# A token difference taken from DRAM in place of a second subtraction in the up projection

## The chip, the cores and the metric

One Trainium2 chip, of which the program uses one core. The core's engines work side by side, each through its own row of instructions: TensorE (PE; its weight loads are listed apart as PEld), VectorE (DVE), ScalarE (ACT), GpSimd (POOL) and SyncE (SP), which here only issues transfers (DMAs). The metric is the device time of one execution in microseconds (us), lower is better.

## The reference

The kernel computes one decoder layer on S = 512 tokens of width D = 1024, all in float32: an RWKV-7 time mix, a sparse attention (compressed, selected and window branches), and a gated feed-forward part of width F = 2816 with a short convolution over the tokens. Only the last part is touched by the change. In short form:

```python
h = rmsnorm(x, norm_ffn)              # 512 x 1024
p = h @ W_up                          # 512 x 5632: gates and values
u = causal_conv(p, taps=3) + bias     # over the tokens
y = silu(u[:, :F]) * u[:, F:]         # 512 x 2816
out = x + rmsnorm(y @ W_down, g)      # 512 x 1024
```

## The kernel before

**Numbers.** TensorE multiplies in a reduced format. So each float32 operand is split into a high part (a copy by ACT) and a low part (operand minus high part, by DVE or POOL), and each product is three: high x high, low x high, high x low.

**Up projection.** `W_up` is cut into 44 blocks of 128 columns, which the loop takes as 22 pairs `j` (a gate and a value block). Pairs 0 to 9 are plain products. Pairs 10 to 21 (the tuple `SEVEN`) are computed by `seven(j)`: a 2 x 2 block product from seven products in place of eight, whose weight sums are made ahead and whose results `sg` and `sv` are put together by additions on DVE (`add`, L1572) from TensorE's sums `st`, `su` and so on. The weights for all this come from DRAM (`sw...r`, L168), are split by ACT (L134) and by DVE or POOL (L172), and lie in a pool `sw` with rings of buffers (`sraw` has four).

Behind each pair come the convolution (L1619 to L1621), the gate, the product `y` (L1635), and its split into `ah[:, j]` (ACT, L1638) and `al[:, j]` (DVE, L1639), two tiles that stay in SBUF for the down projection. `lft` and `rgt` are tokens 0 to 255 and 256 to 511.

**Down projection.** It, too, is a 2 x 2 block product from seven (L1749, `down`): the blocks are the two halves of the tokens by the first and last 11 pairs (`KH` = 11). It needs differences of `y` between the blocks. The first, T1 = `y[rgt] - y[lft]` for pairs 0 to 10, takes the place of `y[rgt]` in the up loop (L1637), before the split; so `ah` and `al` hold T1's high and low part. For pairs 11 to 21 the loop then makes T2 = `y[rgt] - T1` of the pair 11 earlier and T4 = `y[lft] - T2`. T2 takes two subtractions, of T1's high part (L1647) and of its low part (L1648), T4 one (L1649). Both lie in one tile `t24` (two buffers in a pool `t2`) and are stored to DRAM, `t24d` (pairs 11 to 20 by SP, L1645, one iteration later; pair 21 by POOL, L1652). The down projection loads them back as `t` (`load` in `turn`, L1706).

**Down weights.** `down_w` (L1655) loads the weights in the order in which they are used, `dw0`, `dw1`, ...: a load (L1668, SP), a high part (L1668, ACT) and a low part (L1669; POOL for n = 1, 4, 7, 10, ..., DVE otherwise). From n = 3 on the parts are `hh` and `hl`, eight slots. The first ten are started before the up loop is done. Behind them the pools `t2`, `sw` and others are closed, and a pool `ep` opens on the same memory. A tile of `ep` waits for the last use of the tile that lay there. `dw10r` to `dw13r` are the first loads in it. From n = 10 on `keep` pins the order in which loads and splits stand in each engine's row; the rest is put in order by a scheduler.

Of the kernel before, what the change touches and what calls it, by code (L numbers as in the profile page):

```python
# [10 lines left out]
F32 = mybir.dt.float32  # L11
F32R = mybir.dt.float32r
AF = mybir.ActivationFunctionType
OP = mybir.AluOpType
# [14 lines left out]
SEVEN = (10, 11, 12, 13, 14, 15, 16, 17, 18, 19, 20, 21)  # L29
SGRP = 2  # L30
UPOS = {j: i for i, j in enumerate(SEVEN + tuple(sorted(set(range(22)) - set(SEVEN))))}
RB = 4
KH, TL = 11, 4
# [19 lines left out]
def hybrid_layer(ctx: ExitStack, tc: tile.TileContext, a, out, dbg=None, stop=None):  # L53
# [3 lines left out]
    def pool(name, side="left", c=None):  # L57
        p = tc.tile_pool(name=name, bufs=1, side=side, reuse_waits="tile")
        if c is None:
            return p  # L60
        return c.enter_context(p)
# [192 lines left out]
    def weight_sums():  # L254
        gs = [group_sums(x, f) for x, f in zip(SGROUPS, fsum)]
        for i in range(0, len(gs), 4):
            for _ in range(8):
                for y in gs[i:i + 4]:
                    next(y)
                    yield  # L260

    t24d = dr.tile([KH, 128, S], F32, name="t24d", bufs=1)
    dsum = [[dr.tile([k.stop - k.start, 128, 512], F32, name=f"ds{i}{k.start}", bufs=1) for i in range(4)] for k in DCH]

# [1214 lines left out]
    with pool("ff") as ff:  # L1479
# [11 lines left out]
        def token_forms():  # L1491
            with pool("tr", "left") as tr_:
                raws = [{(r, n): tr_.tile([128, 2, 256], F32, tag=f"tr{r}{n}", name=f"tr{c}{r}{n}", bufs=1)
                         for r in range(2) for n in range(2)} for c in range(2)]

                def load(c, r, n):
                    ks = slice(2 * c, 2 * c + 2)
                    keep(ve.tensor_tensor(raws[c][r, n], quarter(h2h, r, n)[:, ks].bitcast(F32),
                                          quarter(h2l, r, n)[:, ks].bitcast(F32), op=OP.add))

                def diff(c, o, x, y):
                    keep(ve.tensor_tensor(raws[c][o], raws[c][x], raws[c][y], op=OP.subtract))

                def high(c, i, o):
                    keep(sc.activation(forms[i][0][:, 2 * c:2 * c + 2], raws[c][o], AF.Copy))

                def low(c, i, o):
                    keep(ve.tensor_tensor(forms[i][1][:, 2 * c:2 * c + 2], raws[c][o],
                                          forms[i][0][:, 2 * c:2 * c + 2].bitcast(F32), op=OP.subtract))

                for c in range(2):
                    load(c, 0, 1)
                    load(c, 0, 0)
                    diff(c, (0, 0), (0, 1), (0, 0))
                    yield
                    high(c, 0, (0, 0))
                    load(c, 1, 1)
                    diff(c, (0, 1), (0, 1), (1, 1))
                    yield
                    high(c, 2, (0, 1))  # L1520
                    low(c, 0, (0, 0))
                    diff(c, (1, 1), (1, 1), (0, 0))
                    load(c, 1, 0)
                    yield
                    high(c, 1, (1, 1))
                    low(c, 2, (0, 1))
                    diff(c, (1, 0), (1, 0), (1, 1))
                    yield
                    high(c, 3, (1, 0))
                    low(c, 1, (1, 1))  # L1530
                    low(c, 3, (1, 0))
                    yield
            yield
# [10 lines left out]
            return hi, lo  # L1544

        def form_seq():
            for j in SEVEN:
                n = SEVEN.index(j)
                fs = [f[n % SGRP] for f in fsum[n // SGRP]]
                for x, eng in (((0, 0), po), (2, po), (1, ve), (3, po), ((0, 1), po), (4, po), ((1, 1), ve)):  # L1550
                    src = fs[x - 1] if isinstance(x, int) else a["up4"][x[0], x[1], UPOS[j]]
                    ahead.append(form_w(src, f"sw{j}{x if isinstance(x, int) else 5 + 2 * x[0] + x[1]}", eng))
                    yield
# [4 lines left out]
        def seven(j):  # L1558
# [29 lines left out]
            add(v[:, lft], t[1][:, rgt], u2)  # L1588
            return g, v

        side = token_forms()
        sctx2 = ExitStack()
        for j in range(22):
            us = []
            sv_ = None
            if j == 2:
                sw = pool("sw", "right", sctx2)
            if j == SEVEN[0]:
                for _ in side:
                    pass  # L1600
            if j in SEVEN:
                sv_ = seven(j)
            for x in range(2):
                blk = 2 * j + x
                if blk < NU:
                    p = pu4[blk]
                    half_up(blk, 1)
                elif sv_ is not None:
                    p = sv_[x]
                else:  # L1610
                    wh, wl = after.get(blk) or split_w(upw(blk), f"up{blk}")
                    p = ((pj, px, py, pz)[blk % 4] if j < SEVEN[0] else pj)(f"pu{blk}")
                    mm3(p, wslice(wh), wslice(wl), lambda k: h2h[:, k, :], lambda k: h2l[:, k, :])
                if blk == 2 * SEVEN[0] - 1:
                    for _ in range(5):
                        next(coming)
                cv = blk * 4
                u = fu.tile([128, S], F32, tag=f"u{x}", name=f"u{blk}", bufs=2)
                sc.activation(u, p, AF.Identity, scale=cvec[:, cv + 2:cv + 3], bias=cvec[:, cv + 3:cv + 4])  # L1619
                ve.scalar_tensor_tensor(u[:, 1:], p[:, :S - 1], cvec[:, cv + 1:cv + 2], u[:, 1:], op0=OP.mult, op1=OP.add)  # L1620
                ve.scalar_tensor_tensor(u[:, 2:], p[:, :S - 2], cvec[:, cv:cv + 1], u[:, 2:], op0=OP.mult, op1=OP.add)  # L1621
                us.append(u)
                if j < SEVEN[0]:
                    for _ in range(1):
                        next(side, None)
                if (j > 2 or x == 0 if j < SEVEN[0] else x == 0 and j < 19):
                    next(ws, None)
            if sv_ is None:
                sc.activation(us[0], us[0], AF.Silu)
                (ve if j > SEVEN[0] - 3 else po).tensor_tensor(us[1], us[0], us[1], op=OP.mult)  # L1630
                y = us[1]
            else:
                sc.activation(sv_[0], us[0], AF.Silu)
                y = sv_[1] if j >= KH else us[1]
                ve.tensor_tensor(y, us[1], sv_[0], op=OP.mult)  # L1635
            if j < KH:
                ve.tensor_tensor(y[:, rgt], y[:, rgt], y[:, lft], op=OP.subtract)  # L1637
            sc.activation(ah[:, j, :], y, AF.Copy)  # L1638
            ve.tensor_tensor(al[:, j, :], y, ah[:, j, :].bitcast(F32), op=OP.subtract)  # L1639
            if j >= KH:  # L1640
                if j == KH:
                    t2ctx = ExitStack()
                    t2 = pool("t2", "left", t2ctx)
                else:
                    sy.dma_start(t24d[j - 1 - KH], t24)  # L1645
                t24 = t2.tile([128, S], F32, tag="t24", name=f"t24{j}", bufs=2)
                ve.tensor_tensor(t24[:, lft], y[:, rgt], ah[:, j - KH, rgt].bitcast(F32), op=OP.subtract)  # L1647
                ve.tensor_tensor(t24[:, lft], t24[:, lft], al[:, j - KH, rgt].bitcast(F32), op=OP.subtract)  # L1648
                ve.tensor_tensor(t24[:, rgt], y[:, lft], t24[:, lft], op=OP.subtract)  # L1649
            if j == 1:  # L1650
                f4ctx.close()
# [3 lines left out]
        def down_w(f, k):  # L1655
            n = next(ring)
            src = a["down4"][f[0], f[1], k] if isinstance(f, tuple) else dsum[k // 2][f][k % 2]
            if n < WB:
                hi, lo = (wp.tile([128, 512], F32R, tag=t, name=f"dw{t}{n}", bufs=WB) for t in ("whi", "wlo"))
            else:  # L1660
                hi, lo = (y[:, (n - WB) % 8, :] for y in (h2h, h2l))
            if n < 8 or n > 9 and n % 8 < 2 or n % 8 >= 6:
                raw = wp.tile([128, 512], F32, tag="raw", name=f"dw{n}r", bufs=RAWB)
            elif n < 10:
                raw = t2.tile([128, 512], F32, tag="draw", name=f"dw{n}r", bufs=2)
            else:
                raw = ep.tile([128, 512], F32, tag="draw", name=f"dw{n}r", bufs=4)
            load, high = sy.dma_start(raw, src), sc.activation(hi, raw, AF.Copy)  # L1668
            low = (po if n % 3 == 1 else ve).tensor_tensor(lo, raw, hi.bitcast(F32), op=OP.subtract)  # L1669
            if n >= 10:  # L1670
                keep(load)
                keep(high)
                keep(low)
            return hi, lo
# [244 lines left out]
```

## Time and profile before

| what | value |
|---|---|
| median of three runs | 1137.72 us (1138.17, 1132.95, 1137.72) |
| the profiled execution | 1133.54 us |
| span of its trace | 1131.5 us |
| mean granted TensorE clock | 0.997 |
| instructions | 21237 |
| moved by DMA | 208.33 MB, 184 GB/s |

The up projection's pairs 11 to 21 lie between about 905 and 1029 us, and the down projection's first product starts at 1018.99. In rows of the profile L12 is line 12 of the kernel, `out<-in` the tiles with buffer numbers left out, `x3` a count. SPq, ACTq and so on are issues of DMAs by an engine's queue. A value in brackets behind a row is the idle time ahead of it and the instruction that ended it. A view of a line or a tile also gives the time from the issue of a DMA to its landing.

### The profile page before, as it was taken

Reading aid. Unit: us, or ns where it says so; the run is one execution under the profiler, and the core shown is the slowest. Engines: PE = TensorE matmul, PEld = TensorE weight load, DVE = VectorE, ACT = ScalarE, POOL = GpSimd, SP = SyncE. Lnnn points to the kernel's source line nnn. Section 1 sums busy time; section 2 is a strip of 40 time slices with the busy share of each in tenths; the row PEclk is TensorE's granted clock in tenths of the full one; section 3 lists DMA queues with packets and bytes.
Section 4 is the critical chain, followed back from the end, with each engine's and each line's share of the span. In section 5 each row is a group of like instructions: output and inputs, shape, how many; then the busy total and the mean of one; then the engine's idle time right before and its main releaser. Section 6 shows DMA issues by size and latency. Waiting matters only on the chain.

```text
span 1131.5 us, 21237 instructions
## 1 busy us (share of the span) xinstructions
PE 1110.3 (98%) x7704; PEld 909.6 (80%) x7704; DVE 750.4 (66%) x1432; ACT 639.2 (56%) x1258; POOL 613.5 (54%) x615
## 2 busy tenths in 40 slices
PE   9999999999999999999999999999999999999997
PEld 7888888877888887766666777888888899998885
DVE  4236664735666552597787754755785699997986
ACT  6447763554666434386675654543554576665554
POOL 4346674535666453566545543540578777753431
PEclk9999999999999999999999999999999999999999
DMA  7524468632666896516576465777568678968783
GB/s 256 144 81 124 141 166 217 182 104 86 182 146 172 235 242 216 132 48 194 171 218 181 127 149 166 231 240 220 136 185 202 207 263 227 266 181 302 228 283 113
DMA packets 117002, 208.33 MB, mean 184 GB/s; under 512 B 37025, under 2 KB 39905, under 8 KB 110754
## 3 DMA queue, kind: packets, MB, share of 16 engines
q1 hardware_dynamic: 93538, 144.05, 40.6%
q0 software_dynamic: 7504, 48.50, 18.4%
q10 hardware_dynamic: 15856, 14.42, 4.0%
q8 instruction: 61, 1.00, 0.4%
q14 instruction: 43, 0.35, 0.1%
HBM read 179.60 MB, written 72.35 MB: 223 GB/s over the span
## 4 chain that ended last, share of the span: by engine, by line
PE 87%; DVE 5%; DMA 3%; POOL 2%; issue 1%; ACT 1%; SPq 0%; DVEq 0%; POOLq 0%; ACTq 0%
PE st L1567 4%; PE sg L1567 3%; PE dn L1745 3%; PE dn L1746 3%; PE dn L1747 3%; PE gt L348 3%; PE o L1218 3%; PE gt L349 3%; PE gt L350 3%; PE pt L150 3%; PE ub L1276 3%; PE pu L234 2%; PE ub L1278 2%; PE pu L232 2%; PE pu L233 2%; PE ub L1277 2%
## 5 line engine op out<-in xcount | busy, mean ns | idle before, releaser
L1166 ACT ACTIVATE p<-p,stt 128x384 f32<-128x384 f32 (+3 forms) x128 | 70.6, 554 | 33.4 <-DVE stt L1164 30.8
L1164 DVE CUSTOM_DVE_ANT_0 p<-s,rh 128x384 f32<-128x384 f32 (+3 forms) x128 | 59.2, 484 | 21.5 <-PE s L1150 17.9
L1138 POOL TENSOR_SCALAR p<-p,stt 128x512 f32<-128x512 f32 (+1 forms) x64 | 39.3, 622 | 38.7 <-DVE stt L1131 24.5
L1746 PE MATMUL dn<-hl,ah 128*128 128x512 f32 x148 | 57.6, 389 | 0.0
L1747 PE MATMUL dn<-hh,al 128*128 128x512 f32 x148 | 57.6, 389 | 0.0
L1745 PE MATMUL dn<-hh,ah 128*128 128x512 f32 x148 | 57.2, 389 | 0.0
L150 PE MATMUL pt<-ident,p 128*128 128x128 f32 x320 | 44.3, 273 | 1.2 <-DVE p L1140 1.2
L1157 PE MATMUL s<-kst,qs 128*128 128x512 f32 (+1 forms) x128 | 38.8, 394 | 5.8 <-DVE stt L1164 5.6
L150 PEld LDWEIGHTS pt<-ident,p 128*128 128x128 f32 x320 | 37.8, 141 | 6.9 <-DVE p L1140 1.6
L1218 PE MATMUL o<-PT,vt 128*64 128x384 f32 (+3 forms) x256 | 41.0, 443 | 0.0
L1209 ACT ACTIVATE PT<-pt 128x512 f32<-128x512 f32 x48 | 27.5, 587 | 10.4 <-PE pt L150 10.3
L1157 PEld LDWEIGHTS s<-kst,qs 128*128 128x128 f32 x128 | 21.2, 189 | 15.0 <-DVE stt L1164 11.8
L1140 DVE TENSOR_SCALAR p<-p,stt 128x512 f32<-128x512 f32 (+1 forms) x64 | 32.3, 532 | 0.7
L1747 PEld LDWEIGHTS dn<-hh,al 128*128 128x128 f32 x148 | 27.8, 188 | 5.8
L1745 PEld LDWEIGHTS dn<-hh,ah 128*128 128x128 f32 x148 | 27.8, 188 | 5.8
L1746 PEld LDWEIGHTS dn<-hl,ah 128*128 128x128 f32 x148 | 27.8, 188 | 5.7
L1218 PEld LDWEIGHTS o<-PT,vt 128*64 128x64 f32 x256 | 16.3, 136 | 18.3 <-issue 16.0
L272 POOL DMA_DIRECT2D ds<-in_down_dram x36 | 25.6, 710 | 7.3 <-DMA ds<-ds 7.3
L1620 DVE SCALAR_TENSOR_TENSOR u<-pu,cvec,u 128x511 f32<-128x511 f32 x20 | 15.0, 748 | 19.2 <-ACT u L1619 19.2
L1211 DVE COPY PT<-pt 128x512 f32<-128x512 f32 x32 | 21.8, 680 | 8.6 <-PE pt L150 8.5
L251 POOL DMA_DIRECT2D fs<-in_up_dram x36 | 26.0, 731 | 0.5 <-issue 0.4
L868 ACT ACTIVATE UV<-xs 64x256 f32<-64x256 f32 x16 | 6.0, 378 | 35.7 <-PE xs L861 35.3
(2206 smaller groups left out, 4242.4 us busy)
## 6 DMA issues: line engine op xcount, KB each, us to landing
fs<-in_up_dram POOLq DMA_DIRECT2D x36, 512.0 KB, 6.5
ds<-in_down_dram POOLq DMA_DIRECT2D x30, 512.0 KB, 6.1
fs<-fs POOLq DMA_DIRECT2D x12, 512.0 KB, 4.4
ds<-ds POOLq DMA_DIRECT2D x10, 512.0 KB, 5.7
gtd<-gt ACTq DMA_DIRECT2D x16, 256.0 KB, 4.8
qs<-qd SPq DMA_DIRECT2D x32, 128.0 KB, 3.6
g<-gtd SPq DMA_DIRECT2D x16, 256.0 KB, 3.6
t24d<-t SPq DMA_DIRECT2D x10, 256.0 KB, 5.4
```

The costliest lines, as they stand in the source:

```text
L150: return te.transpose(o, i, ident)
L348: te.matmul(p, wh(k), hh[:, k, :], start=k == 0, stop=False)
L349: te.matmul(p, wh(k), hl[:, k, :], start=False, stop=False)
L1138: po.tensor_scalar(o.pe[e, b, k], o.pe[e, b, k], w, 1.0, op0=OP.mult, op1=OP.mult)
L1157: m = te.matmul(s_[:, :n], qt, kt[:, x, b, :n], start=x == 0, stop=x == 1)
L1164: ve.tensor_tensor_reduce(sb, parts[b], rh[e][:, (3 - qb) * 128:], -1.0, BIG, OP.add, OP.min, st[e][:, 0, i:i + 1])
L1166: sc.activation(sb, sb, AF.Exp, scale=-1.0, bias=st[e][:, 0, i:i + 1], accum_out=st[e][:, 1, i:i + 1])
L1218: te.matmul(acc[e * 64:e * 64 + 64, j * 128:], vt[:, j, b * 256 + g * 64:b * 256 + g * 64 + 64], m[e][:, c:c + n], start=False, stop=k == ...
L1567: te.matmul(p, w[y][:, ks], x[z][:, k, :], start=first and k + n == 0, stop=last and k == hf - 1 and n == 2, skip_group_check=True)
L1745: te.matmul(p, xh, w[0], start=first, stop=False)
L1746: te.matmul(p, xh, w[1], start=False, stop=False)
L1747: te.matmul(p, xl, w[0], start=False, stop=last)
```

## The change

T1 of pairs 0 to 10 is also stored in DRAM as float32 (`t1d`, 11 tiles of 128 x 256) by ACT, behind the split into `ah`. For pairs 11 to 21 SP loads it back into two buffers `t1` of pool `t2`: two loads at pair 11, then one in each pair, for the pair after next. T2 is then one subtraction, `y[rgt] - t1`. The raw tiles of `dw8` and `dw9`, which had two buffers in `t2`, now use the ring `sraw`.

The diff also lets pairs outside `SEVEN` come behind it (`plain`, the branch in `form_seq`). `SEVEN` is unchanged, so this code doesn't run.

```diff
+    t1d = dr.tile([KH, 128, 256], F32, name="t1d", bufs=1)
     t24d = dr.tile([KH, 128, S], F32, name="t24d", bufs=1)
...
+        def t1_load(k):
+            t = t2.tile([128, 256], F32, tag="t1", name=f"t1{k}", bufs=2)
+            sy.dma_start(t, t1d[k])
+            return t
+
...
-            if j in SEVEN:
-                sv_ = seven(j)
+            if j >= SEVEN[0]:
+                sv_ = (seven if j in SEVEN else plain)(j)
...
             sc.activation(ah[:, j, :], y, AF.Copy)
+            if j < KH:
+                tc.keep_in_program_order(sc.dma_start(t1d[j], y[:, rgt]))
             ve.tensor_tensor(al[:, j, :], y, ah[:, j, :].bitcast(F32), op=OP.subtract)
             if j >= KH:
                 if j == KH:
                     t2ctx = ExitStack()
                     t2 = pool("t2", "left", t2ctx)
+                    t1s = [t1_load(0), t1_load(1)]
                 else:
                     sy.dma_start(t24d[j - 1 - KH], t24)
                 t24 = t2.tile([128, S], F32, tag="t24", name=f"t24{j}", bufs=2)
-                ve.tensor_tensor(t24[:, lft], y[:, rgt], ah[:, j - KH, rgt].bitcast(F32), op=OP.subtract)
-                ve.tensor_tensor(t24[:, lft], t24[:, lft], al[:, j - KH, rgt].bitcast(F32), op=OP.subtract)
+                ve.tensor_tensor(t24[:, lft], y[:, rgt], t1s[j - KH], op=OP.subtract)
+                if j < 20:
+                    t1s.append(t1_load(j - KH + 2))
                 ve.tensor_tensor(t24[:, rgt], y[:, lft], t24[:, lft], op=OP.subtract)
...
             elif n < 10:
-                raw = t2.tile([128, 512], F32, tag="draw", name=f"dw{n}r", bufs=2)
+                raw = sw.tile([128, 512], F32, tag="sraw", name=f"dw{n}r", bufs=4)
```

What this does to the rows of the engines is seen in their order in the built programs, before and after. The numbers behind tile names are those of buffers, and lines are those of each kernel. First DVE, around the end of pair 11; `t` is the tile of T2 and T4, or behind the arrow that of T1, and `sv_10122` and `sv_10134` hold `y`. Before:

```order
L1639 TENSOR_TENSOR al<-sv_10122,ah 128x512
L1647 TENSOR_TENSOR t_10275<-sv_10122,ah 128x256
L1572 TENSOR_TENSOR sv_10280<-st_10282,su_10284 128x256
L1648 TENSOR_TENSOR t_10275<-t_10275,al 128x256
L1649 TENSOR_TENSOR t_10275<-sv_10122,t_10275 128x256
L1572 TENSOR_TENSOR sg_10279<-sg_10279,su_10284 128x256
```

After:

```order
L1665 TENSOR_TENSOR al<-sv_10134,ah 128x512
L1674 TENSOR_TENSOR t_10291<-sv_10134,t_10287 128x256
L1578 TENSOR_TENSOR sv_10297<-st_10299,su_10301 128x256
L1677 TENSOR_TENSOR t_10291<-sv_10134,t_10291 128x256
L1578 TENSOR_TENSOR sg_10296<-sg_10296,su_10301 128x256
```

One row goes, behind the next pair's `sv`; the others keep their order. Then SP at the end of the up projection, with the semaphores that each row waits for in brackets. `DMAHW` counts transfers of the hardware's queues, `DMASW` those that POOL issued. Before:

```order
L168 DMA sw218r<-in_up_dram 128x512 [waits DMAHW6_49,Pool_49]
L1668 DMA dw2r<-in_down_dram 128x512 [waits DMAHW7_49,DVE_49]
L1668 DMA dw3r<-in_down_dram 128x512 [waits DMAHW0_49,Pool_49]
L1645 DMA t24d<-t_11522 128x512 [waits DMAHW1_49,DVE_49]
L1668 DMA dw4r<-in_down_dram 128x512 [waits DMAHW2_49,DVE_49]
L1668 DMA dw5r<-in_down_dram 128x512 [waits DMAHW0_49,DMAHW3_49,DVE_49,Activation_49]
L1668 DMA dw6r<-in_down_dram 128x512 [waits DMAHW5_49,DMAHW4_49,Pool_49]
L1668 DMA dw7r<-in_down_dram 128x512 [waits DMAHW2_49,Pool_49]
L1645 DMA t24d<-t_11677 128x512 [waits DMAHW6_49,DVE_49]
L1668 DMA dw10r<-in_down_dram 128x512 [waits DMAHW7_49,DMAHW6_49]
L1668 DMA dw11r<-in_down_dram 128x512 [waits PE_49]
```

After:

```order
L168 DMA sw218r<-in_up_dram 128x512 [waits DMAHW1_49,Pool_49]
L1696 DMA dw8r<-in_down_dram 128x512 [waits DMAHW3_49,DMAHW2_49,Pool_49]
L1696 DMA dw9r<-in_down_dram 128x512 [waits DMAHW6_49,Pool_49]
L1696 DMA dw2r<-in_down_dram 128x512 [waits DMAHW4_49,DVE_49]
L1612 DMA t_11548<-t1d 128x256 [waits DMAHW5_49,DVE_49]
L1672 DMA t24d<-t_11546 128x512 [waits DVE_49]
L1696 DMA dw3r<-in_down_dram 128x512 [waits DMAHW7_49,Pool_49]
```

and four rows (`dw4r` to `dw7r`) further on:

```order
L1672 DMA t24d<-t_11702 128x512 [waits DMAHW4_49,DVE_49]
L1696 DMA dw10r<-in_down_dram 128x512 [waits DMAHW5_49,DMAHW6_49,DMASW0_49,DVE_49]
L1696 DMA dw11r<-in_down_dram 128x512 [waits PE_49]
```

`dw8r` and `dw9r`, which stood in SP's row at about 853 us, now stand ahead of `dw2r`, and a T1 load stands ahead of the store of each `t24d`, where `dw3r` stood before. `dw10r` has two more waits. `DMASW0` at the count that it asks for is the landing of POOL's store of pair 21's tile, and `DVE` the subtraction that fills that tile. In both programs `dw10r` lies at the same address; before, pair 20's `t24` tile lay there, and now pair 21's does, since the two `t1` buffers are given their places in `t2` first.

More of the change, by code (lines that the diff above doesn't have):

```diff
@@ L1546, in form_seq @@
         def form_seq():
-            for j in SEVEN:
+            for j in range(SEVEN[0], 22):
+                if j not in SEVEN:
+                    for b, c, eng in ((0, 0, po), (0, 1, ve), (1, 0, po), (1, 1, ve)):
+                        ahead.append(form_w(a["up4"][b, c, UPOS[j]], f"sw{j}{b}{c}", eng))
+                        yield
+                    continue
                 n = SEVEN.index(j)
@@ L1589, in seven, with plain @@
             return g, v
+        def plain(j):
+            g, v = (pj if j % 2 else px)(f"sg{j}"), (pj if j % 2 else py)(f"sv{j}")
+            for p in (g, v):
+                for i in range(2):
+                    w = ahead.pop(0)
+                    for k in range(hf):
+                        ks = slice(k * 128, k * 128 + 128)
+                        for n, (y, z) in enumerate(((0, h2h), (0, h2l), (1, h2h))):
+                            te.matmul(p, w[y][:, ks], z[:, i * hf + k, :], start=i + k + n == 0,
+                                      stop=i == 1 and k == hf - 1 and n == 2)
+                    next(coming, None)
+            return g, v
+        def t1_load(k):
+            t = t2.tile([128, 256], F32, tag="t1", name=f"t1{k}", bufs=2)
+            sy.dma_start(t, t1d[k])
+            return t
         side = token_forms()
```

## The prediction

> **What bounds the kernel now.** The first thing to read is the profile page's busy table: how full is each engine over the whole span?
>
> ```profile
> span 1131.5 us, 21237 instructions
> PE 1110.3 (98%) x7704; PEld 909.6 (80%) x7704; DVE 750.4 (66%) x1432; ACT 639.2 (56%) x1258; POOL 613.5 (54%) x615
> ```
>
> PE (TensorE's matmuls) works 98% of the time, DVE (VectorE) 66%. An instruction taken off DVE is worth only the PE time that waits for DVE. So the next view is that of the waits, for PE and its weight loads, from 800 us to the end:
>
> ```profile
> PE st L1567 <- DVE sv L1572: 1.6, 3, 0.7
> PE pu L234 <- POOL up5l L172: 0.7, 1, 0.7
> ```
>
> ```profile
> PEld st L1567 <- DVE sv L1572: 2.5, 4, 0.9
> ```
>
> The second fence is the weight loads' largest. Columns are total us, times and longest. PE's list is complete: three waits for VectorE's `sv` addition in the up projection, one for POOL (GpSimd), and none in the down projection. Where they lie is shown by 20 us windows over the second half of the pairs (length, then busy us of PE, PEld, DVE, ACT, POOL, granted clock, DMA share, GB/s):
>
> ```profile
> 940.00:960.00 20.00, 19.97 (x171) 19.74 (x170) 18.65 (x33) 13.15 (x24) 12.99 (x11) 1.00 0.84 240
> 960.00:980.00 20.00, 19.04 (x162) 18.64 (x161) 18.93 (x33) 13.52 (x24) 15.87 (x14) 1.00 0.97 269
> 980.00:1000.00 20.00, 20.00 (x174) 19.96 (x173) 18.33 (x33) 13.31 (x24) 13.78 (x11) 1.00 0.86 263
> 1000.00:1020.00 20.00, 19.31 (x161) 18.92 (x161) 19.34 (x34) 13.11 (x24) 9.38 (x7) 1.00 0.46 137
> ```
>
> DVE is 92 to 97% busy here and ACT (ScalarE) 66%. PE is idle 0.03 + 0.96 + 0 + 0.69 = 1.68 us; with the weight load that has to start again behind each wait, 2.5. I put what a faster DVE can give back at 3.0 at most (2.5 and some small gaps, an estimate).
>
> **One subtraction less.** The removed line, and two of its eleven (pairs 18 and 19) that took long:
>
> ```profile
> L1648 DVE TENSOR_TENSOR t<-t,al x11: 407/425/1514, 925.1 to 1028.4; 128x256 f32<-128x256 f32 x11
> 996.75 1.51 DVE L1648 TENSOR_TENSOR t<-t,al 128x256 f32<-128x256 f32 x1
> 1007.49 1.49 DVE L1648 TENSOR_TENSOR t<-t,al 128x256 f32<-128x256 f32 x1
> 1007.62 0.38 PE L1567 MATMUL st<-tf3h,sw208h 128*128 128x256 f32 x1 [0.69 <-DVE sv L1572]
> 966.68 0.39 PE L1567 MATMUL st<-tf3h,sw168h 128*128 128x256 f32 x1 [0.35 <-DVE sv L1572]
> 977.28 0.39 PE L1567 MATMUL st<-tf3h,sw178h 128*128 128x256 f32 x1 [0.61 <-DVE sv L1572]
> 949.11 7.27 DMA sw166r<-in_up_dram
> ```
>
> The eleven take 0.41 to 1.51 us each, 8.4 in all by the page's group (11 x 763 ns). The other first subtraction (L1647) stays, with another operand. Of PE's three waits the one at 1007.62 goes: the 1.51 us at 996.75 stand ahead of it in DVE's queue, with 0.46 us of idle between. I give it 0.69 plus a restart, and small ones, together 1.3 us. The waits at 966.68 and 977.28 (0.96 together) I leave: by the chain, `sw166r`'s landing of 7.27 us stands ahead of them, and no subtraction shortens that. So PE comes to the down projection **1.3 us** earlier (bounds 0 and 3.0).
>
> **Eleven stores on ACT.** The nearest row is ACT's other DMA issue:
>
> ```profile
> L521 ACTq DMA_DIRECT2D gtd<-gt x16: 326/326/356, 164.6 to 384.4; - x16
> 860.00:890.00 30.00, 30.00 (x134) 24.86 (x133) 14.67 (x17) 14.20 (x23) 22.76 (x21) 1.00 0.83 207
> qs<-qd SPq DMA_DIRECT2D x32, 128.0 KB, 3.6
> ```
>
> 11 x 0.326 = 3.6 us on an engine that in the first pairs is 47% busy (14.20 of 30) while PE waits for nothing: 0 on the path. Without that cover it would cost 0.33 in each pair. The loads: a 128 KB load lands in 3.6 us (`qs<-qd`), each is issued two pairs, some 20 us, ahead of its use. 22 transfers of 128 KB are 2.9 MB; at the 269 GB/s that the fullest window moves this is 10.7 us of DMA, 0.49 a transfer, in a stage with a DMA share of 0.83 to 0.97. I take 0; the upper bound is that the two waits behind loads double, +1.0, and below it is nothing, since no transfer goes.
>
> **Two raw tiles elsewhere.** The loads of `dw8r` and `dw9r` now stand just ahead of `dw2r` on SP (SyncE, which issues the loads), in buffers that POOL reads last here:
>
> ```profile
> 1004.46 1.29 POOL L172 TENSOR_TENSOR sw213l<-sw213r,sw213h 128x512 fp32r<-128x512 f32 x1
> 1006.33 0.33 SPq L1668 DMA_DIRECT2D dw2r<-in_down_dram  x1
> ```
>
> The buffers are free at 1005.75, and `dw2r` was issued at 1006.33 anyway: 0, or at most two issues (0.66) for SP, which waits between them. The rows of six loads now behind a T1 load get one issue more each, 0.33 against some microseconds of landing: 0.
>
> **The wait that appears.** The order of SP's queue shows one edit which the diff doesn't. With two T1 buffers ahead in its pool, the pool's other tiles lie elsewhere, and `dw10r`, the first tile of the pool that opens on that memory, now lies on the last T24 tile (pair 21's), not on pair 20's. So SP holds `dw10r`, and everything behind it, until POOL's store of pair 21's tile has landed. Rows of before, in the order of that new chain:
>
> ```profile
> 1021.79 0.33 SPq L1668 DMA_DIRECT2D dw10r<-in_down_dram  x1
> 1028.35 0.42 DVE L1648 TENSOR_TENSOR t<-t,al 128x256 f32<-128x256 f32 x1
> 1028.81 0.42 DVE L1649 TENSOR_TENSOR t<-sv,t 128x256 f32<-128x256 f32 x1
> 1029.60 0.61 POOL L1652 DMA_DIRECT2D t24d<-t  x1 [7.03 <-DVE t L1649]
> 1027.16 0.63 ACT L1668 ACTIVATE hh<-dw10r 128x512 fp32r<-128x512 f32 x1
> 1030.23 1.30 POOL L1669 TENSOR_TENSOR hl<-dw10r,hh 128x512 fp32r<-128x512 f32 x1
> 1032.60 0.62 PE L1745 MATMUL dn<-hh,ah 128*128 128x512 f32 x2
> 1033.05 0.39 PE L1746 MATMUL dn<-hl,ah 128*128 128x512 f32 x1
> ```
>
> Before, the load was out at 1021.79, 7.8 us ahead of that store. PE wants the high part (`hh`) at 1032.60 and the low part (`hl`) at 1033.05, and the low part was done at 1030.23 + 1.30 = 1031.53, a slack of 1.52. Two landings have to be priced, the store's and the load's:
>
> ```profile
> DMA to landing us min/median/max: 3.0/3.0/3.0
> DMA to landing us min/median/max: 6.6/6.6/6.6
> DMA to landing us min/median/max: 2.8/5.9/14.2
> DMA to landing us min/median/max: 2.5/3.6/8.4
> out_dram<-x2b SPq DMA_DIRECT2D x8, 256.0 KB, 2.0
> 1029.60:1033.00 3.40, 3.40 (x16) 2.82 (x16) 3.40 (x2) 1.12 (x2) 3.16 (x3) 1.00 0.89 292
> 1033.00:1036.30 3.30, 3.30 (x16) 2.71 (x16) 3.23 (x4) 1.40 (x3) 1.84 (x1) 1.00 1.04 400
> ```
>
> In this order: `dw10r`; this very store; POOL's accumulating transfers (L272); all loads of L1668. The store took 6.6 us, but in windows where DMA was 0.89 and 1.04 busy with `dw12r` to `dw17r` and a T24 load, which now stand behind it on SP and can't be in flight. A store of the same size in quiet took 2.0 (`out_dram`). I take 2.8, the least of POOL's queue, nearer to the quiet row, and 3.0 for the load. Then, with the times of before: store issued 1029.60 - 0.46 (the step from 1028.35 to 1028.81 goes) = 1029.14; landed 1031.94; load landed 1034.94; high part +0.63 = 1035.57; low part +1.30 = 1036.87; four hand-overs of about 0.1: 1037.2. That is 4.15 later than 1033.05. DVE's relief moves the chain by the two L1648 of pairs 19 and 20 (1.49 and about 0.42 = 1.9) earlier: 1035.3. The end moves by 1035.3 - 1033.05 = **+2.3**; PE, 1.3 early, would stand 2.4 us for the high part and, after two matmuls, 1.1 for the low one.
>
> [...]
>
> Bounds of this term: 2.0 and 2.5 for the two landings give +1.0; no relief of the chain gives +4.2; and the loads of `dw11r` to `dw17r`, now out some 8 us later and in one bunch, may cost up to 1.5 more: 4.2 + 1.5 = +5.7. Everything else being 0, the profiled execution goes from 1133.54 (span 1131.5 and 2.04 around it) to 1135.8. It stands 4.18 below the median of the runs, 1137.72; on that level the forecast is **1140.0**.
>
> **Rivals.** (1) *The store is as slow as it was, and the clock falls* (slower). With 6.6 in place of 2.8 the chain ends 3.8 later: +6.1, and PE's first gap grows to 6.2 us. The clock's rows at the end of PE's work and at its start:
>
> ```profile
> 1123.50:1128.50 5.00, 0.38 (x2) 0.00 (x0) 4.59 (x10) 1.10 (x4) 0.00 (x0) 1.00 0.59 218
> 1128.50:1129.00 0.50, 0.00 (x0) 0.00 (x0) 0.00 (x0) 0.00 (x0) 0.00 (x0) 0.71 0.99 365
> 10.00:11.00 1.00, 1.00 (x3) 0.56 (x3) 1.00 (x3) 1.00 (x3) 1.00 (x1) 0.50 1.02 406
> 12.00:13.00 1.00, 1.00 (x7) 0.76 (x5) 0.78 (x2) 0.58 (x2) 0.66 (x1) 0.72 1.06 402
> ```
>
> PE's last two matmuls fill the first 0.38 us of the first window, so end at 1123.88; the granted clock is full to 1128.5 and falls within the next half microsecond, so after about 4.7 us idle. At the start it was half for some 3.4 us, which would cost 1.7 us of work. It decides once the store takes over about 5.1 us (gap over 4.7): then +4.6 to +6.1, and 1.7 for the clock, with a bunch of late loads up to +9. That is 1144 to 1147. For it: 6.6 is the only row of this store. Against it: the traffic that slowed it is now behind it. The fall may also come sooner than after 4.7, which the start and the end of the trace don't exclude for a gap between others: with a store of 3.8 the gap is 3.4, and +3.3 for the wait and 1.7 for the clock give 1142.7. [...]
> (2) *The relief wins*: the wait is covered, because DVE's chain of pairs 19 to 21 moves by more than 1.9 or both landings are short, and PE keeps what it gains, -3.0 to 0: 1134.7 to 1137.7. For it: DVE is 92 to 97% busy, so all later work moves up. Against: the chain needs 4.15 us.
> (3) *The change doesn't do what it says*: T1 comes late, and DVE waits for it as it did for nothing before; with 3.6 us of landing against 20 it would take a load of 6 times the median. PE would then wait up to some microseconds in a pair: 1141 to 1147.
>
> **How the numbers follow.** Forecast 0.60 (+1.0 to +5.7, so 1138.7 to 1143.4, likeliest 1140.0; 0.05 of it for a clock that falls early, 1142.7), rival 1 0.20, rival 2 0.17, rival 3 0.03. Half a per cent, 5.7 us, is about what can be told from no change. Within it lie the forecast and nearly all of rival 2; beyond it rival 1 (0.20) and a third of rival 3 (0.01): slower 0.21. Of rival 2 I give 0.04 to a gain of over 5.7, past its bound, if gaps of PE that I don't count go too: faster 0.04. The rest, 0.75, is the same. The range takes rival 2 in with some of the spread of the three runs (1132.95 to 1138.17), from 1133.0, and rival 1 up to 1147.0.
>
> **What the profile after would show.** Right: `dw10r` issued at about 1030 behind POOL's store; a PE wait at the eleventh step of the down projection, split between ACT's high part and POOL's low part, 3 to 4 us in all; the wait at 1007 gone, those at 966 and 977 still there; a store landing in 2 to 3.5; clock 1.00 throughout. Wrong: a landing of 5 or more with a lower clock behind it; no PE wait there (the wait is covered); or DVE waiting for the T1 loads in pairs 11 to 21.

## The result, and the profile after

| | before | after |
|---|---|---|
| median of six runs | 1137.16 us (1132.95 to 1138.17) | 1143.04 us (1141.38 to 1145.31) |
| ratio, 95% interval | | 1.0058 [1.0038, 1.0078] |
| the profiled execution / its span | 1133.54 / 1131.5 | 1144.24 / 1142.4 |

The change costs about 6.6 us (0.0058 x 1137). The forecast was +2.3, the slower rival +6.3 to +9. The busy table of the profile after:

```profile
span 1142.4 us, 21300 instructions
PE 1116.7 (98%) x7704; PEld 912.5 (80%) x7704; DVE 738.3 (65%) x1421; ACT 639.3 (56%) x1258; POOL 612.7 (54%) x615
```

DVE has 12 us less work (8.4 were counted), and PE is 6.4 us longer busy with the same 7704 matmuls. PE's waits from 800 us on (total, times, longest):

```profile
PE st L1573 <- DVE sv L1578: 2.4, 3, 1.2
PE dn L1773 <- ACT hh L1696: 1.9, 1, 1.9
PE pu L234 <- POOL up5l L172: 0.7, 1, 0.7
PE dn L1774 <- POOL hl L1697: 0.6, 1, 0.6
PE dn L1774 <- DVE hl L1697: 0.2, 1, 0.2
```

The waits for `sv` are not fewer than before (1.6, three times), and three rows for the down projection are new. The first two stand where the prediction put them. The chain, from the timeline of after (start, length, idle before and what ended it), and the landings of POOL's store and of `dw10r`:

```profile
1034.06 0.61 POOL L1680 DMA_DIRECT2D t24d<-t  x1 [5.97 <-DVE t L1677]
1036.49 0.33 SPq L1696 DMA_DIRECT2D dw10r<-in_down_dram  x1
1039.22 0.63 ACT L1696 ACTIVATE hh<-dw10r 128x512 fp32r<-128x512 f32 x1 [7.04 <-DMA dw10r<-in_down_dram]
1039.90 0.73 PE L1773 MATMUL dn<-hh,ah 128*128 128x512 f32 x2 [1.90 <-ACT hh L1696]
1041.26 0.80 PE L1774 MATMUL dn<-hl,ah 128*128 128x512 f32 x1 [0.62 <-POOL hl L1697]
```

```profile
DMA to landing us min/median/max: 2.4/2.4/2.4
DMA to landing us min/median/max: 2.6/2.6/2.6
```

So the new wait is there, step by step, with a store of 2.4 (2.8 was taken) and a load of 2.6 (3.0). And the clock fell behind it (columns as in the prediction; the clock is the third number from the end):

```profile
1038.00:1040.00 2.00, 0.10 (x2) 0.10 (x1) 0.00 (x0) 0.74 (x2) 0.06 (x1) 1.00 1.00 382
1040.00:1042.00 2.00, 1.38 (x4) 0.85 (x5) 1.45 (x2) 1.52 (x3) 1.20 (x1) 0.74 0.96 337
1042.00:1043.00 1.00, 1.00 (x4) 0.81 (x3) 0.36 (x1) 0.46 (x2) 0.67 (x1) 0.50 0.80 291
1043.00:1044.00 1.00, 1.00 (x4) 0.72 (x4) 0.54 (x1) 0.94 (x2) 0.61 (x1) 0.50 1.04 354
1044.00:1045.00 1.00, 1.00 (x5) 0.82 (x4) 0.84 (x2) 0.75 (x2) 0.00 (x0) 0.81 0.92 301
```

**Where the time lies.** The starts of one instruction in both timelines can be compared. The difference is 4.1 us already near 796 us, ahead of the first T1 store (813 us in after), and 4.10 at pair 10: the profiled execution of before was one of the quick ones, and this part says nothing about the change. So from here on stretches are compared, not absolute times. The first matmul of the down projection, DVE's first subtraction `tt` of T24's turn, and PE's last matmul, before and after:

```profile
1018.99 0.40 PE L1745 MATMUL dn<-dwwhi,ah 128*128 128x512 f32 x1
1045.65 1.21 DVE L1712 TENSOR_TENSOR tt<-ah,t 128x1024 f32<-128x1024 f32 x1
1123.49 0.39 PE L1747 MATMUL dn<-hh,al 128*128 128x512 f32 x1
```

```profile
1024.22 0.40 PE L1773 MATMUL dn<-dwwhi,ah 128*128 128x512 f32 x1
1056.62 1.21 DVE L1740 TENSOR_TENSOR tt<-ah,t 128x1024 f32<-128x1024 f32 x1
1134.12 0.39 PE L1775 MATMUL dn<-hh,al 128*128 128x512 f32 x1
```

From pair 10's last weight (`sw116h`, at 914.24 and 918.34) to the first `dn` PE needs 104.75 us before and 105.88 after (+1.13); from there to the end of its last matmul 104.89 and 110.29 (+5.40). With 4.10 from earlier and 0.27 in the tail these are the 10.9 between the spans. The down projection is where the change costs, and pairs 11 to 21 don't give back the 1.3 that were forecast.

At the eleventh step itself PE loses 4.52 us (the matmuls there are 5.24 us late ahead of it and 9.76 late at the second step behind it): 2.06 until the high part, 0.91 until the low part, 1.55 by matmuls at half clock. The other 0.88 come 30 us later, where PE is held by low parts of weights that DVE makes (the row of 0.2 above is one). That looks like the whole story: the forecast's 3.6 for the stall, plus a clock that fell. The experiments say that there is a second limit close behind it.

### The profile page after: what moved, and what is told of

Read it like the earlier page. It is cut to its first block, busy times and chain, and to the rows that moved or that the text cites. A ratio compares the mean times of both kernels' runs of the same rounds, so it can differ in the third digit from the quotient of the medians.

```text
span 1142.4 us, 21300 instructions
## 1 busy us (share of the span) xinstructions
PE 1116.7 (98%) x7704; PEld 912.5 (80%) x7704; DVE 738.3 (65%) x1421; ACT 639.3 (56%) x1258; POOL 612.7 (54%) x615
## 4 chain that ended last, share of the span: by engine, by line
PE 74%; DVE 10%; DMA 7%; ACT 3%; issue 3%; POOL 3%; SPq 0%; DVEq 0%; ACTq 0%; POOLq 0%
PE o L1219 3%; PE gt L349 3%; PE pt L150 3%; PE gt L350 3%; PE gt L351 3%; PE ub L1277 3%; PE pu L234 2%; PE ub L1279 2%; PE st L1573 2%; PE pu L232 2%; PE pu L233 2%; PE ub L1278 2%; DVE hl L1697 2%; PE v L349 2%; PE sg L1573 2%
```

## The experiments

For each kernel: the ratio to the kernel before, run beside it on the same chip, and from its profile the two stretches, "pairs" (from `sw116h` to the first `dn`) and "down" (from there to PE's last matmul). All measured stretches at a glance; `dw10r` and `tt` are counted from the first `dn`:

| kernel | ratio, 95% interval | pairs | dw10r out | first tt | tt to end | down |
|---|---|---|---|---|---|---|
| before | 1 | 104.75 | 2.80 | 26.66 | 78.23 | 104.89 |
| after | 1.0058 [1.0038, 1.0078] | 105.88 | 12.27 | 32.40 | 77.89 | 110.29 |
| e1_lay | 1.0036 [1.0017, 1.0055] | 106.84 | 2.06 | 28.93 | 77.91 | 106.84 |
| e2_wait_alone | 1.0060 [1.0039, 1.0080] | 105.56 | 13.20 | 33.39 | 77.88 | 111.27 |
| e3_one_sub | 0.9996 [0.9981, 1.0012] | 102.83 | 1.76 | 25.11 | 79.80 | 104.91 |
| e4_raws_moved | 1.0019 [1.0005, 1.0033] | 104.55 | 2.78 | 27.67 | 77.87 | 105.54 |
| e5_clock_filled | 1.0076 [1.0054, 1.0098] | 105.01 | 12.47 | 33.15 | 77.87 | 111.02 |
| e6_layout_all | 1.0005 [0.9989, 1.0020] | 105.84 | 0.21 | 25.10 | 79.83 | 104.93 |
| e7_t1_on_act | 1.0067 [1.0046, 1.0087] | 111.52 | 8.98 | 29.53 | 77.88 | 107.41 |
| e8_stores_alone | 0.9991 [0.9978, 1.0005] | 103.02 | 1.44 | 25.87 | 79.04 | 104.91 |
| e9_dve_relieved | 1.0063 [1.0046, 1.0081] | 103.42 | 12.26 | 32.87 | 79.78 | 112.65 |
| e10_t1_on_pool | 1.0077 [1.0056, 1.0099] | 117.60 | 8.98 | 30.47 | 77.92 | 108.39 |
| e11_t1_early | 1.0038 [1.0021, 1.0056] | 105.85 | 9.04 | 29.95 | 77.88 | 107.83 |

**e1_lay: the layout put back.**

```diff
                 if j == KH:
                     t2ctx = ExitStack()
                     t2 = pool("t2", "left", t2ctx)
-                    t1s = [t1_load(0), t1_load(1)]
                 else:
                     sy.dma_start(t24d[j - 1 - KH], t24)
                 t24 = t2.tile([128, S], F32, tag="t24", name=f"t24{j}", bufs=2)
+                if j == KH:
+                    t1s = [t1_load(0), t1_load(1)]
```

> The changed kernel with one allocation moved: the first t24 tile takes its place in the pool before the T1 buffers, so that dw10r lies on pair 20's tile as it did; the order of all engines is that of the changed kernel. Theory: of the 6.6 us that the change costs, the wait at the eleventh step of the down projection makes 4.5 (2.1 idle for the high part, 0.9 for the low part, 1.5 by the lower clock behind it) and about 0.8 comes from late weights behind it, so this kernel is 1 to 2 us above the kernel before (ratio 1.001 to 1.002), with no PE wait in the first 15 steps of the down projection and the clock at 1.00 there; the waits for sv in pairs 16 to 21 stay. Rival (the traffic of the T1 transfers makes the weights late in any case): still 4 us or more above, with waits for hh or hl in the down projection.

Measured: +4 us (0.0036 x 1135), what the rival said, and with waits for low parts, but by another cause than the rival's traffic, as e6 shows. The wait at the eleventh step is gone, the mean granted clock is 0.996 (0.994 in after), but "down" is still 1.95 longer than before. SP's timeline shows why, and PE's where it is lost:

```profile
1023.22 0.43 SPq L1697 DMA_DIRECT2D dw12r<-in_down_dram  x1
1029.39 0.33 SPq L1697 DMA_DIRECT2D dw13r<-in_down_dram  x1
1060.76 0.50 PE L1775 MATMUL dn<-hl,ah 128*128 128x512 f32 x1 [0.53 <-DVE hl L1698]
```

SP now stands 6 us at `dw13r`, which in this layout lies on the T1 buffers and waits for pair 21's subtraction. No weight up to there is late for PE; the loss comes 30 us later. This is the first sign that SP's hold acts by something other than `dw10`.

**e2_wait_alone: the wait without the rest of the change.**

```diff
                     t2 = pool("t2", "left", t2ctx)
+                    t24 = t2.tile([128, S], F32, tag="t24", name="t24n", bufs=2)
+                    ve.memset(t24[:, 0:1], 0.0)
```

> The kernel before with its two t24 buffers exchanged by one unused tile (a one-element memset), so that dw10r lies on pair 21's tile: the wait alone, with two subtractions, without T1 transfers and with dw8 and dw9 where they were. Theory: POOL's store lands some 2.4 us after its issue, the load 2.6 after that, so PE stands about 2.8 us for dw10's high part and 0.9 for its low part, and the clock falls for some 1.6: 4.5 to 6.5 us above the kernel before. Rival (the wait costs so much only because the changed kernel's other parts came late): at most 2 us, no fall of the clock.

Measured: +6.8 us (4.4 to 9.1), just above the range expected, "down" 6.38 longer, and the stall as foreseen:

```profile
1038.98 1.22 PE L1747 MATMUL dn<-hh,ah 128*128 128x512 f32 x2 [2.80 <-ACT hh L1670]
```

The wait alone costs as much as the whole change. It needs neither the T1 transfers nor the moved raw tiles. Here PE has lost 3.89 of the 6.38 when `dw10`'s low part is there, 2.30 more while the clock is low (0.50 in each microsecond from 1041 to 1044), and only 0.19 later.

**e3_one_sub: the subtraction alone** (T1's low part is left out of T2 and T4).

```diff
-                ve.tensor_tensor(t24[:, lft], t24[:, lft], al[:, j - KH, rgt].bitcast(F32), op=OP.subtract)
```

> The kernel before without the subtraction of T1's low part (that part is left out of T2 and T4), all else as before: DVE's relief alone. By the prediction PE comes 1.3 us earlier to the down projection (0 to 3.0), the wait near 1007 gone, those near 966 and 977 still there. Rival (the subtraction has slack everywhere): 0, with three waits for sv of the same size.

"pairs" is 1.92 shorter in the profile, but the ratio, 0.9996 [0.9981, 1.0012], leaves anything from 2.2 faster to 1.4 slower. The waits view of pairs 11 to 21 has one wait left where before had three, and two were expected to stay:

```profile
PE st L1567 <- DVE sv L1572: 0.2, 1, 0.2
```

**e4_raws_moved: the raw tiles of dw8 and dw9 alone.**

```diff
             elif n < 10:
-                raw = t2.tile([128, 512], F32, tag="draw", name=f"dw{n}r", bufs=2)
+                raw = sw.tile([128, 512], F32, tag="sraw", name=f"dw{n}r", bufs=4)
```

> The kernel before with the raw tiles of dw8 and dw9 in the ring of sw and nothing else; their loads stand ahead of dw2r. By the prediction 0 (below 0.3). Rival: dw3r comes later, ACT stands for it with pair 21's u behind it, and PE waits for sv in the last pair: 0.5 to 1.0 us above, with a wait near 1017 that the kernel before has not.

Neither: 2 us above (0.6 to 3.7), by the profile 0.65 in "down" and -0.2 in "pairs". `dw3r` is not late (ACT takes it at 1011.33 without idle time). But with no raw tile of `dw9` in their way, `dw12r` to `dw17r` go out at once behind `dw11r`, the T24 load with them, `dw20r` goes out 1.5 us later (15.83 us behind the first `dn` and not 14.37), and the first `tt` comes a microsecond later, at 27.67. The profile accounts for a part of the 2 us only.

**e5_clock_filled: the clock kept up.**

```diff
                     w = begun.pop(0) if begun else down_w(f, k)
+                    if m == 0 and k == KH - 1:
+                        jk = py("jk")
+                        for _ in range(9):
+                            keep(te.matmul(jk, ah[:, k - 1, 0:128], last[0], start=True, stop=True))
```

> The changed kernel with nine matmuls of no use (0.227 us each, 2.04 in all, into a bank that is written anew later) between the tenth and the eleventh step of the down projection, where PE stands 2.06 us for dw10's high part. Theory (the fall of the clock is a cost of its own, 1.5 of the 4.5 us at that place): the granted clock stays at 1.00 from 1038 to 1046, matmuls behind the wait take 0.23 us each and not 0.43, and the kernel is 1.3 to 2.0 us faster than the changed one, so about 4.6 to 5.3 above the kernel before. Rival (behind the wait PE is held by late weights and the clock costs nothing): as the changed kernel, 6.6 above, within 0.5.

The fill did its work, as two windows show:

```profile
1038.00:1040.00 2.00, 0.72 (x3) 0.25 (x2) 0.79 (x1) 1.54 (x3) 1.26 (x1) 1.00 1.00 286
1042.00:1043.00 1.00, 1.00 (x6) 0.82 (x5) 0.87 (x1) 0.96 (x3) 0.61 (x1) 1.00 1.01 291
```

The clock is 1.00 where it was 0.50, and six matmuls stand in a microsecond instead of four. And nothing is gained: the kernel is 8.6 us above the one before (6.1 to 11.1), "down" 111.02. What PE saves here it waits for later:

```profile
1059.55 0.50 PE L1774 MATMUL dn<-hl,ah 128*128 128x512 f32 x1 [0.29 <-DVE hl L1697]
1066.97 0.50 PE L1774 MATMUL dn<-hl,ah 128*128 128x512 f32 x1 [0.33 <-DVE hl L1697]
1073.41 0.50 PE L1774 MATMUL dn<-hl,ah 128*128 128x512 f32 x1 [0.26 <-DVE hl L1697]
```

So the fall of the clock is no cost of its own here: of its 6.13 us in "down" PE loses 3.9 at the eleventh step and 2.2 behind it, at DVE's low parts (in after 4.5 and 0.9, in e1 none and 1.95). The table's column "tt to end" gives the next theory: it is 77.87 to 77.92 in eight kernels, whatever "down" is, and larger where "down" is at its floor of 104.9 (before, e3, e6, e8); e9, below, is the exception. So in these profiles, e9 aside, "down" is the larger of 104.9 and (first `tt`) + 77.9. From the first `tt` on DVE is busy for 46.56 of the next 46.68 us in after (large subtractions, splits and the low parts of the weights in a fixed order), PE waits for low parts in it, and however late it starts, it never catches up.

How the hold of `dw10r` reaches `tt` is seen at `dw18r`, which takes the buffer of `dw10r` and goes out when POOL has made `dw10`'s low part. Before:

```profile
1031.56 0.34 SPq L1668 DMA_DIRECT2D dw18r<-in_down_dram  x1
1044.51 1.23 DVE L1669 TENSOR_TENSOR hl<-dw23r,hh 128x512 fp32r<-128x512 f32 x1 [2.60 <-ACT hh L1668]
```

After:

```profile
1039.94 1.27 POOL L1697 TENSOR_TENSOR hl<-dw10r,hh 128x512 fp32r<-128x512 f32 x1 [5.26 <-ACT hh L1696]
1041.23 0.34 SPq L1696 DMA_DIRECT2D dw18r<-in_down_dram  x1
1055.47 1.23 DVE L1697 TENSOR_TENSOR hl<-dw23r,hh 128x512 fp32r<-128x512 f32 x1 [2.60 <-ACT hh L1696]
```

From the first `dn`, `dw18r` goes out at 12.57 us before and 17.01 after (+4.44), ACT has it at 18.75 and 24.49 (+5.74, since it also lands more slowly: 6.2 us from its issue to ACT before, 7.5 after), and the same 5.7 us stand at `dw23`'s low part, with `tt` right behind it. So PE's stall and DVE's late row are two effects of one hold, and the later of the two sets the end. e1 has the late row without the stall; no run has the stall without the late row.

**e9_dve_relieved: DVE's row shortened**, on top of e5.

```diff
-            low = (po if n % 3 == 1 else ve).tensor_tensor(lo, raw, hi.bitcast(F32), op=OP.subtract)
+            low = (po if (n % 2 == 0 if 23 < n < 40 else n % 3 == 1) else ve).tensor_tensor(lo, raw, hi.bitcast(F32), op=OP.subtract)
```

> e5_clock_filled, and between dw24 and dw39 POOL makes the low part of every second weight in place of every third (three rows less on DVE from the first subtraction tt of the down projection on). Theory (what sets the end of the changed kernel is DVE's row from the first tt on, which starts late because SP stood at dw10r, and needs 77.9 us from there to PE's last matmul in each of the profiles so far but one; the stall and the clock at the eleventh step lie under it): with a shorter row the down projection takes 107.5 to 108.5 us in place of 111.0, no hl wait between 1055 and 1080, 3 us faster than e5_clock_filled, about 5 above the kernel before. Rival (late weight loads, not DVE, make the waits near 1060 to 1073): the down projection stays at 110.5 to 111.5.

(In the table the 77.9 holds in fewer profiles than the expectation says: it is longer wherever "down" is at its floor.) The forecast fails: "down" is 112.65, longer still. The reason is in DVE's row. In after the first `tt` takes 1.21 us (above). Here, DVE and POOL side by side:

```profile
1050.91 1.64 POOL L1697 TENSOR_TENSOR hl<-dw24r,hh 128x512 fp32r<-128x512 f32 x1
1051.32 2.31 DVE L1740 TENSOR_TENSOR tt<-ah,t 128x1024 f32<-128x1024 f32 x1
1059.32 1.75 POOL L1697 TENSOR_TENSOR hl<-dw30r,hh 128x512 fp32r<-128x512 f32 x1
1059.84 2.31 DVE L1740 TENSOR_TENSOR tt<-ah,t 128x1024 f32<-128x1024 f32 x1
```

POOL's added low parts run at the same time as the two `tt`, which take 1.1 us longer each, 2.2 together. "tt to end" grew by 1.91, and PE waits 2.04 for one DVE low part. So the end goes with DVE's row here too, in the wrong direction. The row was not shortened, so the run fits the theory but doesn't test it.

**e6_layout_all: the layout mended altogether**, on top of e1.

```diff
             g3 = ep.tile([128, D], F32, name="gb4")
+            ep.tile([128, 4, 256], F32, tag="tt", name="ttn", bufs=1)
```

> As e1_lay, and the tile tt of the down projection takes its place in the pool ahead of the raw tiles, so that dw10r to dw13r lie neither on T24 nor on T1 tiles; SP's order is that of the changed kernel. Theory: in e1_lay dw13r lay on the last T1 tile and SP stood for it from 1023 to 1029, which cost 1.95 in the down projection; that goes, the 2.1 of pairs 11 to 21 stay, so 2 us above the kernel before (1.5 to 2.7), with no DVE wait for hl near 1060. Rival (late by the traffic of T1 or by dw8 and dw9): down projection still 1.5 to 2 longer than before.

"down" is 104.93, its floor, and the kernel is level with the one before, 1.0005 [0.9989, 1.0020]. In the down projection no wait of PE is left. The 2 us that were expected to remain are not seen: 0.6 by the ratio (-1.2 to 2.3), with "pairs" 1.09 longer by the profile. The cost of the change was its layout.

**e8_stores_alone: the eleven stores by ACT alone.**

```diff
             sc.activation(ah[:, j, :], y, AF.Copy)
+            if j < KH:
+                tc.keep_in_program_order(sc.dma_start(t1d[j], y[:, rgt]))
```

> The kernel before with the eleven stores of T1 by ACT and nothing else (no loads, two subtractions). By the prediction 0 (within 0.5). Rival (the issues on ACT hold the activations behind them): 0.5 to 3.6 above, with PE waits between 800 and 920 that the kernel before has not.

0.9991 [0.9978, 1.0005]: the stores cost at most 0.6 us, as forecast. But "pairs" is 1.73 shorter than before, almost as in e3, without any relief for DVE. So a profile's "pairs" moves by this much for reasons other than DVE's work.

**e7, e10 and e11: the T1 loads elsewhere**, on top of e6.

```diff
+            if KH < j < 21:
+                t1s.append(t1_load(j - KH + 1))
...
-            t = t2.tile([128, 256], F32, tag="t1", name=f"t1{k}", bufs=2)
-            sy.dma_start(t, t1d[k])
+            t = t2.tile([128, 256], F32, tag="t1", name=f"t1{k}", bufs=3)
+            sc.dma_start(t, t1d[k])
...
-                if j < 20:
-                    t1s.append(t1_load(j - KH + 2))
```

This is e7; e10 has `po.dma_start`, e11 `sy.dma_start` there.

> As e6_layout_all, with the T1 loads issued by ACT, one pair ahead, into three buffers, so that SP's order in pairs 11 to 21 is that of the kernel before (with the loads of dw8 and dw9 as in e4_raws_moved). Theory (what eats DVE's relief is the six weight loads held behind a T1 load that waits for DVE): PE reaches the down projection 1.5 to 2 us earlier than in the kernel before, as in e3_one_sub, and the kernel is 0 to 1.5 us faster than the kernel before. Rival (the bytes of T1 themselves slow the weight loads): PE's way through pairs 11 to 21 is 1 to 2 us longer than before, as in the changed kernel.

> e7_t1_on_act with the T1 loads issued by POOL in place of ACT: SP's order nearly that of the kernel before (two pairs of neighbours exchanged), the layout of e6_layout_all. Theory (six weight loads held on SP behind a T1 load eat DVE's relief): pairs 11 to 21 take 102.5 to 104 us of PE, 1 to 2 less than before, and the kernel is level with the one before or up to 1.5 us faster. Rival (the bytes, or the issuing engine's row, wherever the loads are issued): 105.5 or more, as in the changed kernel or in e7.

> e6_layout_all with three T1 buffers and each load written one step earlier in the program, so that a T1 load on SP waits for the subtraction of an earlier pair and not for the one just made; its place in SP's row, ahead of the same weight loads, stays. Theory (SP stands at the T1 load for DVE): pairs 11 to 21 take 103 to 104.5 us of PE, and the kernel is level with the one before or 1 us faster. Rival (it is the place, or the T24 store that moved with it, that holds the weight loads): 105 to 106.8, as in e1 and e6.

All three theories fail: "pairs" takes 111.52, 117.60 and 105.85. The sizes that the rivals of e10 and e11 gave hold (105.5 or more; 105 to 106.8); e7 is longer than either of its two had it. PE's waits between 915 us and the first `dn`, of e7 and of e10:

```profile
PE st L1573 <- DVE sv L1578: 6.4, 6, 2.1
```

```profile
PE st L1573 <- DVE sv L1578: 10.6, 8, 2.0
```

Two weights' low parts of e10 tell how, with what POOL does meanwhile:

```profile
949.51 0.81 POOL L273 DMA_DIRECT2D ds<-in_down_dram  x1
950.06 0.85 POOL L1612 DMA_DIRECT2D t<-t1d  x1
950.29 3.75 DVE L172 TENSOR_TENSOR sw158l<-sw158r,sw158h 128x512 fp32r<-128x512 f32 x1
950.64 1.59 POOL L172 TENSOR_TENSOR sw154l<-sw154r,sw154h 128x512 fp32r<-128x512 f32 x1
```

In before this DVE instruction (`sw158l`) takes 1.47 us, beside one subtraction of POOL's (946.56 to 948.11). With POOL's row shifted so that two subtractions fall on it, in e10 a T1 issue too, it takes 3.75, in e7 3.23, and the next pair's `sv` stands behind it. That this makes all of the 7 and 13 us is not shown. In all three the third T1 buffer also brought `dw10r` onto a T1 tile, so that SP stood until about 9 us into the down projection; by the table's rule the first `tt` at 29.5 to 30.5 gives 107.4 to 108.4, and that is what "down" takes.

## Why the prediction was right and wrong

- **The range and the direction held.** 1143.04 lies in 1133 to 1147 and near the top of the forecast's own part (1138.7 to 1143.4). The size was 2.9 times too small: about 6.6 in place of 2.3. As a difference 6.6 lies above that part's bound of +5.7; that the time still lies inside is in part luck, since the six runs of before have a lower median than the three from which it was reckoned.
- **The wait that appears** was right in its place, its order and its landings: 2.4 and 2.6 (2.8 and 3.0 taken), the high part first, then the low part, 1.90 and 0.62 of idle in the waits. e2 shows that the wait makes the cost by itself, e6 that without it (and without e1's `dw13r`) the cost is gone.
- **The first term that was mis-sized** is the relief of that chain, taken as 1.9. Counted from `sw116h`, POOL's store is issued at 115.36 us before (1029.60 - 914.24) and at 115.72 after (1034.06 - 918.34), where the forecast has 113.0 (1029.14 - 1.9 - 914.24). So the store was 2.7 late. The steps behind it were 0.9 shorter than taken, and the low part reached PE 1.9 later than forecast. The chain follows PE's arrival and not DVE's earlier rows: in seven kernels with one subtraction (after, e1, e5, e6, e7, e9, e11) the store is issued 9.78 to 10.04 us behind the first `dn`, while "pairs" goes from 103.4 to 111.5; in before it is 10.61. So a relief of DVE in pairs 19 and 20 could move it only by moving PE, and PE came 1.1 later and not 1.3 earlier.
- **The second** is what stands behind `dw10r` on SP. It was taken as 0, with "up to 1.5 more" as a bound, and measured 2.4: in "down" PE is 2.97 late when it has `dw10`'s low part and 5.40 at the end. 2.3 + 1.9 + 2.4 = 6.6, and the two stretches grew by 1.13 + 5.40 = 6.5. The prediction priced the path of one weight to PE. The hold also makes the first `tt` 5.74 us late (32.40 against 26.66), and from there the end is fixed at 77.9. In before that row had a slack of 78.23 - 77.87 = 0.36 us, so the row alone gives 5.74 - 0.36 = 5.4. The waits view showed no wait in the down projection, and the prediction read "no wait" as room to spare. Of the 2.4, the matmuls at half clock take 1.55, and e5 shows that with the clock full the row takes as much.
- **The relief of 1.3** for PE is not shown. The waits near 1007 and 966 did go, though the second was to stay; but that near 977 grew from 0.61 to 1.18, and two others came (0.36 and 0.85). "pairs" is 103.4 to 106.8 us in the five kernels with the changed order there (after, e1, e5, e6, e9) and 103.0 to 105.6 in four with the old one (before, e2, e4, e8). Single profiles scatter by more than the term.
- **The six displaced loads and `dw3r`, costed at 0**: one part of this is visible. In four of those five kernels PE waits 0.85 to 0.87 for the last pair's `sv`, and before has no such wait. In after ACT stands for `dw3r`, which went out behind the T1 load and the T24 store and landed in 4.9 us, with pair 21's `u` behind it in ACT's row:

```profile
1016.70 0.63 ACT L1696 ACTIVATE hh<-dw3r 128x512 fp32r<-128x512 f32 x1 [2.96 <-DMA dw3r<-in_down_dram]
1022.75 0.38 PE L1573 MATMUL st<-tf3h,sw218h 128*128 128x256 f32 x1 [0.85 <-DVE sv L1578]
```

- **The two raw tiles, costed at 0**: e4 has them at 2 us by the runs (0.6 to 3.7), of which its profile shows 0.65 in "down", through the same first `tt`.
- **ACT's stores at 0**: right (e8).
- **Rival 1** had about the right size (+6.3 and more) for the wrong reason. The store was quick (2.4 us), not slow. The clock fell early (to 0.50, behind a wait of 1.90 us, where the case given 0.05 has a gap of 3.4), and e5 shows that this was no cost of its own, since DVE's row stood close behind it.
- **Rivals 2 and 3** did not come: the wait is not covered, and in no profile does DVE wait for a T1 load.
- **Open** is what moves "pairs" by 1 to 2 us between kernels that hardly differ there (e3 and e8 against before), and so why PE came no earlier and whether the subtraction is worth anything. e6 puts the change with its layout mended within -1.2 and +2.3 us of the kernel before.

## What to carry to other kernels

A stage whose waits view is empty may still have another engine's row a third of a microsecond behind PE. Before a queue is held for some microseconds, look for the row that is nearly full behind it, and count from its first instruction to the end, in before, how much later it may start. Work taken off an engine's row moves a chain only where the chain waits for that row; look first at what its first instruction waits for. And a new buffer in a pool is an edit to every tile that later opens on that memory: read the waits of the first loads there, not only those of the tiles that the diff names.

## What the runs showed of the hardware

The granted clock can fall after a much shorter idle gap than the 4.7 us that the prediction took from the end of the trace. In after it was 2.06 us (1.90 in the waits), then two matmuls and 0.62 of idle, and the clock was 0.50 from 1041 to 1044 us. Between gaps of the same length it differs, as e10 shows with two of its waits for `sv` (2.0 and 1.9 us):

```profile
947.70:949.70 2.00, 0.05 (x1) 0.00 (x0) 2.00 (x5) 0.94 (x2) 2.00 (x3) 1.00 0.64 176
949.70:951.70 2.00, 1.93 (x16) 1.94 (x17) 2.00 (x4) 1.11 (x2) 2.00 (x3) 1.00 0.98 272
983.40:985.40 2.00, 0.18 (x2) 0.00 (x0) 2.00 (x5) 1.26 (x2) 2.00 (x3) 1.00 0.54 157
985.40:987.40 2.00, 1.91 (x9) 1.91 (x10) 1.16 (x4) 0.78 (x1) 2.00 (x3) 0.55 1.05 306
```

Of nine waits of 1.9 to 2.1 us in after, e7, e9 and e10 the clock fell behind four (to 0.50 in after, e7 and one of e10's, 0.55 in the two microseconds behind the other of e10's) and was 1.00 behind five. What tells them apart is not shown.

The same VectorE subtraction took longer or shorter with other work of GpSimd beside it. The first `tt` took 1.21 us in after, where POOL's `hl<-dw25r` began 0.25 us behind it and itself took 2.11 (`hl<-dw22r`, the one before, 1.30). In e9 the two `tt` took 2.31 each, and POOL's low part in the rows above began 0.41 and 0.52 us ahead of them. `sw158l` took 1.47 us beside one subtraction of POOL's (before), and 3.23 (e7) and 3.75 (e10) beside two. In e9 the work moved from VectorE to GpSimd so cost VectorE more than it saved: with three rows less DVE is busy for 741.0 us, in e5 for 738.5.
